# Row power of the last norm: ScalarE's root and a Newton step on VectorE in place of GpSimd's power

## The chip, the cores and the metric

The kernel runs on one core of a Trainium2 chip. A core has five engines with a queue each: TensorE (PE, matmuls; its weight loads are shown apart as PEld), VectorE (DVE), ScalarE (ACT), GpSimd (POOL) and SyncE (SP, which here issues DMAs). The metric is the device time of one execution in microseconds (us), median of several runs.

## The reference

One layer over 256 tokens of width 2048: a gated feed-forward network (hidden width 5632), a mixer (a recurrence and a pooling branch), and a second feed-forward network, each between norms. What matters here is the second network and the norm behind it, which make the output:

```python
def _rmsnorm(x, g):
    xf = x.astype(jnp.float32)
    y = xf * lax.rsqrt(jnp.mean(xf * xf, axis=-1, keepdims=True) + NORM_EPS)
    return (y * g.astype(jnp.float32)).astype(x.dtype)

f = _swiglu(_rmsnorm(h, ln_ffn2_pre[l]), ffn2_gate[l], ffn2_up[l], ffn2_down[l])
h = h + MACARON_WEIGHT * _rmsnorm(f, ln_ffn2_post[l])
```

Each token (a row) needs one number for its last norm: the reciprocal root of the mean square of its 2048 values of `f`. All is float32.

## The kernel before

**Matmuls.** A float32 product is made of three matmuls on split operands: high times high, low times high, high times low (`mm3`, L273 to L275). ScalarE makes the high part by a cast (`wH`, `kH` of weights, `xH` of activations), VectorE the low part by a subtraction (`wL`, `kL`, `xL`). The 256 tokens are two halves of 128 rows (`h` = 0 and 1). Weights stream in by DMAs that SP issues. In most of the blocks some products are joined in the manner of Strassen (`seven`, L458), which takes further sums on VectorE (`t`, `sf`, `u`).

**The order of work.** PE, ACT and DVE instructions stand in an order that the program writes itself: pieces of work are given as jobs with an engine ("A" ScalarE, "V" VectorE, "G" GpSimd, "D" an SP DMA), a planned duration, a due time and what they follow; `play` (L168) runs them against a small model of the engines and emits them in that order. An instruction that an engine reaches early waits for semaphores and holds all behind it on that engine.

**The end of a feed-forward network.** `post` (L996) forms the down projection in blocks of 512 columns and the norm behind it. The evacuation of a block (`ev_of`, L1008) squares and sums its 512 columns on ScalarE (`sumsq`, L845, into `ss[h][:, c]`) and multiplies it by the gain on VectorE (`scale`, L1016, into `fg`). For the first three blocks the sum, times a factor and with epsilon, is made ahead (`some`, L1029 and L1031, `part[h]`, in the profile `rp`). The last block's sums are ordered so that half 0 is done some 11 us before half 1. `last` (L1039) then has, for each half:

- `norm` (VectorE, L1044): `r2 = ss * kf + part`, one number per row; in the profile `rt`
- `power` (GpSimd, L1048): `r = r2 ^ -0.5`; in the profile `rs`
- `out` (VectorE, L1052), four times: `fg * r + residual` for 512 columns each, and behind each one a DMA of 256 KB to the output (SP, L1851)

`post` is called for both feed-forward networks and for the mixer's output, so there are six powers in `post`; two of them (the second network's) stand at the very end. GpSimd's only other work late in the program is DMA issue: the last of these loads the residual (`h<-hsp`, L1830). Behind the last instruction of the program each engine has closing instructions that the compiler adds (a DRAIN, a barrier over all engines); the profile puts them at the line that closes the program, L1895.

**ScalarE's functions.** ScalarE loads a table ahead of some functions (ACT_TABLE_LOAD). Before the change it does so eight times in the program, the last time for the SiLU of the second network (L858, at 1338 us); the kernel has no root on ScalarE.

Of the kernel before, what the change touches and what calls it, by code (L numbers as in the profile page):

```python
# [13 lines left out]
AF = mybir.ActivationFunctionType  # L14
ALU = mybir.AluOpType
# [3 lines left out]
P = 128  # L19
# [4 lines left out]
NKF = DFF // P  # L24
# [27 lines left out]
DOWN = ((0, "fffffffffqffffqfflqlllqllqllqllqlllll", 0),  # L52
        (2, "fffqffqffqffqffqffqflqllqlll", TRAIL))
# [13 lines left out]
class Node:  # L67
    __slots__ = ("n", "eng", "dur", "fn", "due", "lag", "give", "ready", "left", "kids")

    def __init__(s, *a):  # L70
        s.n, s.eng, s.dur, s.fn, s.due, s.lag, s.give = a
        s.ready, s.left, s.kids = 0.0, 0, []
# [8 lines left out]
class Block:  # L81
    def __init__(s, tc, ctx):
        s.tc = tc
        s.nc = nc = tc.nc
        E = ctx.enter_context
        s.n = 0
        s.nxt = None
        s.late, s.after = [], []
        s.clk, s.order, s.asks, s.freed, s.jobs = 0.0, [], {}, {}, []
        s.cp = E(tc.tile_pool(name="cp", bufs=1))  # L90
        s.wp = E(tc.tile_pool(name="wp", bufs=3))
        s.up = E(tc.tile_pool(name="up", bufs=NUNITS))
        s.tp = E(tc.tile_pool(name="tp", bufs=TB))
        s.sp = E(tc.tile_pool(name="sp", bufs=4))
        s.dp = E(tc.tile_pool(name="dp", bufs=1, space=bass.MemoryType.DRAM))
        s.pm = E(tc.tile_pool(name="pm", bufs=4, space=PSUM))
        s.pt = E(tc.tile_pool(name="pt", bufs=4, space=PSUM))
        s.ident = s.const([P, P], "ident")
        make_identity(nc, s.ident)
        s.mhalf = s.const([P, 16], "mhalf")  # L100
        nc.gpsimd.memset(s.mhalf, -0.5)

    def nm(s, p):
        s.n += 1
        return f"{p}_{s.n}"
# [741 lines left out]
    def ffn(s, wg, wu, wd, uT, uj, rs, gpost, resid, emit, reload, xs=None):  # L847
        nc = s.nc
        at = s.T_at(uT)
        nb = NKF // 4  # L850
        hT, hX, hj = [None] * nb, [None] * nb, [None] * nb
        def evs(b, r):
            sig, sj, T1, tj = [None, None], [None, None], [], []

            def silu(h, get, deps, t):
                def f():
                    sig[h] = s.tmp("sg")
                    nc.scalar.activation(out=sig[h], in_=get(), func=AF.Silu, scale=r[h])  # L858
                sj[h] = s.job("A", 0.59, f, t, (*deps, b < 2 and uj[h]))
                return sj[h]  # L860

            def silu_in(h, get, deps, t):
                def f():
                    sig[h] = get()
                    nc.scalar.activation(out=sig[h], in_=sig[h], func=AF.Silu)
                sj[h] = s.job("A", 0.59, f, t, deps)
                return sj[h]

            def turned(h, get, j, t):
                def f():  # L870
                    if not T1:
                        T1.append(s.unit(p="T1"))
                    s.turn(T1[0], h, get())
                tj.append(s.job("V", 0.61, f, t, (j,)))
                if h == 1:
                    hj[b] = s.carry(T1, hT, b, tj, t + 12, None, hX)
                return tj[-1]

            def times(h, get, deps, t):
                def f():  # L880
                    nc.vector.scalar_tensor_tensor(out=sig[h], in0=get(), scalar=r[h],
                                                   in1=sig[h], op0=ALU.mult, op1=ALU.mult)
                j = s.job("V", 0.665, f, t, (*deps, sj[h]))
                turned(h, lambda: sig[h], j, t + 6)
                return j

            def times_in(h, get, deps, t):
                def f():
                    nc.vector.tensor_tensor(out=get(), in0=get(), in1=sig[h], op=ALU.mult)
                j = s.job("V", 0.602, f, t, (*deps, sj[h]))  # L890
                return turned(h, get, j, t + 1)
            return silu, times, silu_in, times_in

        silu, times, _, _ = evs(0, rs)
        if xs:
            pss = s.head(wg, 0, NKD, at, *xs[:2], uT)
            xs[2]()
            for h in range(2):
                s.freed[f"f{h}"] = silu(h, lambda h=h: pss[f"f{h}"], (), 14)
        else:  # L900
            s.lead(wg, 0, at, NKD, silu, lambda k, h: uj[k // 4, h])
        while s.after:
            s.after.pop(0)()
        s.gemm(wu, 0, at, 0, NKD, NKD, times, ("l0", "l1"))
        rb, rj = s.spread(rs, uj)
        nT, nj, nx = s.normed(uT, rb, rj, s.clk + 4, xs and xs[1])
        silu, times, _, _ = evs(1, rs)
        s.gemm(wg, 512, at, 0, NKD, NKD, silu, ("f0", "f1"))
        s.gemm(wu, 512, at, 0, NKD, NKD, times, ("l0", "l1"))
        nq = max(o.count("q") for o in FAST.values())  # L910
        su = Sums(nq)
        t = s.clk + 6
        for q, m in ((0, 2), (2, 1), (3, 1), (4, 1), (5, 1))[:nq - 1]:
            s.sums(nx, su, q, m, t + 4 * q, (nj[q // 2][0],))
        kd = lambda k: (nj[k // 4][1],)
        for b in range(2, nb):
            _, _, silu, times = evs(b, [1.0, 1.0])
            s.seven(wg, b * 512, wu, b * 512, s.T_at(nT), NKD, su, FAST[b], silu, times,
                    kd=kd)
        s.post(wd, s.T_at(hT), NKF, gpost, 0.5, resid, emit, reload, hT, hj, DOWN, hX)  # L920

    def spread_now(s, rs, out):

# [69 lines left out]
            nj.append((b, s.job("V", va(1024), low, t_ + 5, (c,))))  # L993
        return nT, nj, nx

    def post(s, wd, at, KT, gpost, fac, resid, emit, reload, hT, hj, plan, hX=None):  # L996
        nc = s.nc
        gb = [s.unit(p="gb") for _ in range(2)]
        fg = [[s.unit(p="fg") for _ in range(2)] for _ in range(2)]
        ss = [s.small(4, "ss") for _ in range(2)]  # L1000
# [4 lines left out]
        part, sj = [None, None], {}  # L1005
        kf = 1.0 / (D * fac ** 2)

        def ev_of(c):  # L1008
# [30 lines left out]
            def last(h, scale, a, deps, t):  # L1039
                r = s.small(1, "rs", bufs=8)  # L1040
                r2 = s.small(1, "rt2", bufs=2)

                def norm():
                    nc.vector.tensor_scalar(out=r2, in0=ss[h][:, 3:4], scalar1=kf,  # L1044
                                            scalar2=part[h], op0=ALU.mult, op1=ALU.add)

                def power():
                    nc.gpsimd.tensor_tensor(out=r, in0=r2, in1=s.mhalf[:, :1], op=ALU.pow)  # L1048

                def out(q):  # L1050
                    o = cc_(fg[h], q)
                    nc.vector.scalar_tensor_tensor(out=o, in0=o, scalar=r, in1=resid(h, q),  # L1052
                                                   op0=ALU.mult, op1=ALU.add)
                b = s.job("V", 0.13, norm, t, (a, sj[h, "p"]))
                c = s.job("G", 0.55, power, t, (b,), lag=0.35)
                d = s.job("V", 0.602, scale, t + 0.1, deps)
                sj[h, 3] = d
                for q in range(4):
                    o = s.job("V", 0.665, lambda q=q: out(q), t + 0.2 + 0.1 * q, (c, sj[h, q]))
                    emit(h, q, cc_(fg[h], q), o, s.clk + 0.7 + TURNS[h][q])  # L1060
                return s.job("N", 0, None, 0, (a, d))
            return ev
        xj = list(hj)
        if hX is not None:
            c, o, _ = plan[0]
            t, n, first = s.clk, o.count("q"), {}
# [11 lines left out]
        t, q, js = s.clk, 0, []  # L1078
        for c, o, trail in plan:
            n = 0  # L1080
            for ch in o or "p" * (KT // 2) * (1 + (trail > 0)):
# [5 lines left out]
                    n += 1  # L1087
                t += (21 if ch == "q" else 12) * MM
        n1 = None
        for c, o, trail in plan:  # L1090
            if o:
                use = s.seven(wd, c * 512, wd, c * 512 + 512, at, KT, sm, o, ev_of(c),
                              ev_of(c + 1), trail, kd)
                if n1 is None and own is not None:
                    n1 = o.count("q")
                    for q in range(n1, len(sm)):
                        for k in (2 * q, 2 * q + 1):
                            s.link(use[k], js[q // 2])
            elif trail:
                pss = {}  # L1100
                s.gemm(wd, c * 512, at, 0, KT - trail, KT, None, ("l0", "l1"), kd, pss)
                s.halves(wd, c * 512, at, KT - trail, KT, KT, ("l0", "l1"), pss,
                         lambda k, h: kd(k)[0], lambda h, e: ev_of(c)(h, lambda: pss[f"l{h}"],
                                                                   (e,), s.clk))
            else:
                s.gemm(wd, c * 512, at, 0, KT, KT, ev_of(c), ("f0", "f1"), kd)
# [793 lines left out]
```

## Time and profile before

| | |
|---|---|
| time, median of 3 runs | 2015.26 us (2014.19 to 2015.28) |
| profiled execution: its own time | 2014.53 us |
| profiled execution: span, first to last instruction | 2012.8 us |
| time outside the span (2014.53 less 2012.8) | 1.7 us |
| TensorE busy | 1997.0 us (99%) |
| VectorE busy | 1764.8 us (88%) |
| ScalarE busy | 1200.2 us (60%) |
| GpSimd busy | 339.8 us (17%) |

The page of the profile counts matmuls, vector work and the like as busy. Waits, branches, DMA issues and DRAINs are the sequencers' (PEq, ACTq, DVEq, POOLq, SPq) and are not busy time, though they lie within the span. The chain on the page is followed back from the last working instruction, so what stands behind that instruction is in no share of it and has to be looked up by its line, L1895. In a timeline a row has the start and the duration in us; in brackets stands how long the engine had been idle and what released it. In a view by line, three durations are the least, the median and the longest, in ns.

### The profile page before, as it was taken

What the parts mean: (1) busy time and instruction counts of PE and PEld (TensorE: products, weight loads), DVE (VectorE), ACT (ScalarE), POOL (GpSimd) and SP (SyncE); (2) the same over time, 40 slices, a digit from 0 to 9 for tenths busy, and PEclk for the clock granted to TensorE, in tenths of its full rate; (3) what the DMA queues carried; (4) which work ended last, traced back from release to release, by engine and by line L of the source; (5) the groups of instructions that cost most, each with busy time, mean ns of one, the idle gap of its engine ahead of it and who ended that gap; (6) DMA issues with size and microseconds to landing.
All of it is one profiled execution on the core that took longest, in us unless ns stands there. A gap on an engine that the chain in (4) does not pass through costs nothing.

```text
span 2012.8 us, 28601 instructions
## 1 busy us (share of the span) xinstructions
PE 1997.0 (99%) x9936; PEld 1651.9 (82%) x9936; DVE 1764.8 (88%) x2362; ACT 1200.2 (60%) x1599; POOL 339.8 (17%) x689
## 2 busy tenths in 40 slices
PE   9999999999999999999999999999999999999997
PEld 7888888888888888888788788888888888888886
DVE  6999999999998857789689678679999999999885
ACT  7556666566655656775575444565556655756553
POOL 0131112211000113403220120002211131110000
PEclk9999999999999999999999999999999999999999
DMA  9777777766667777757466567766777877666674
GB/s 331 235 217 230 230 242 222 236 185 211 216 205 255 238 203 211 211 176 214 141 182 183 160 218 240 254 219 180 220 228 225 256 218 231 195 215 209 206 258 142
DMA packets 230305, 435.09 MB, mean 216 GB/s; under 512 B 25104, under 2 KB 28688, under 8 KB 230160
## 3 DMA queue, kind: packets, MB, share of 16 engines
q1 hardware_dynamic: 205008, 387.18, 59.9%
q0 software_dynamic: 24864, 45.95, 8.4%
q8 instruction: 78, 1.28, 0.3%
q14 instruction: 67, 0.55, 0.1%
q10 hardware_dynamic: 288, 0.14, 0.0%
HBM read 398.79 MB, written 8.39 MB: 202 GB/s over the span
## 4 chain that ended last, share of the span: by engine, by line
PE 97%; DVE 1%; issue 1%; ACT 1%; DMA 0%; SPq 0%; POOL 0%; DVEq 0%; POOLq 0%; ACTq 0%
PE mm L273 27%; PE mm L275 26%; PE mm L274 26%; PE ms L275 5%; PE ms L274 5%; PE ms L273 5%; PE pA L1596 0%; PE tr L750 0%; DMA w<-in_ffn_gate_dram 0%; PE mc L732 0%; DVE fg L1052 0%; PE pU L1692 0%; DVE wL L298 0%; DVE xL L759 0%; PE pSa L1704 0%
## 5 line engine op out<-in xcount | busy, mean ns | idle before, releaser
L273 PE MATMUL mm<-wH,xH 128*128 128x512 f32 (+1 forms) x1711 | 668.8, 391 | 0.0
L274 PE MATMUL mm<-wL,xH 128*128 128x512 f32 (+1 forms) x1711 | 663.2, 388 | 0.8 <-DVE wL L250 0.8
L275 PE MATMUL mm<-wH,xL 128*128 128x512 f32 (+1 forms) x1711 | 663.4, 388 | 0.3 <-DVE xL L759 0.3
L275 PEld LDWEIGHTS mm<-wH,xL 128*128 128x128 f32 x1711 | 321.2, 188 | 66.8 <-DVE xL L759 0.7
L273 PEld LDWEIGHTS mm<-wH,xH 128*128 128x128 f32 x1711 | 321.3, 188 | 66.3 <-ACT wH L249 0.3
L274 PEld LDWEIGHTS mm<-wL,xH 128*128 128x128 f32 x1711 | 321.5, 188 | 64.6 <-DVE wL L250 1.1
L292 ACT CAST wH<-w 128x1024 fp32r<-128x1024 f32 x251 | 262.6, 1054 | 174.8 <-PE mm L275 122.9
L298 DVE TENSOR_TENSOR wL<-w,wH 128x1024 fp32r<-128x1024 f32 x251 | 301.3, 1218 | 58.3 <-ACT wH L292 56.7
L530 ACT CAST wH<-t 128x1024 fp32r<-128x1024 f32 x163 | 171.8, 1054 | 194.5 <-DVE t L515 69.6
L250 DVE TENSOR_TENSOR wL<-w,wH 128x1024 fp32r<-128x1024 f32 (+2 forms) x159 | 188.2, 1192 | 74.4 <-ACT wH L249 73.0
L781 POOL DMA_DIRECT2D x<-T x352 | 173.3, 511 | 434.4 <-DVE T L768 238.0
L249 ACT CAST wH<-w 128x1024 fp32r<-128x1024 f32 (+2 forms) x159 | 162.7, 1027 | 135.6 <-PE mm L275 113.6
L534 DVE TENSOR_TENSOR wL<-t,wH 128x1024 fp32r<-128x1024 f32 x163 | 196.1, 1216 | 17.3 <-ACT wH L530 17.0
L530 ACT CAST wH<-w 128x1024 fp32r<-128x1024 f32 (+1 forms) x161 | 132.9, 826 | 120.7 <-PE mm L275 68.8
L273 PE MATMUL mm<-kH,xH 128*128 128x512 f32 x449 | 175.5, 391 | 0.0
L275 PE MATMUL mm<-kH,xL 128*128 128x512 f32 x449 | 174.9, 389 | 0.0
L274 PE MATMUL mm<-kL,xH 128*128 128x512 f32 x449 | 174.7, 389 | 0.0
L534 DVE TENSOR_TENSOR wL<-w,wH 128x1024 fp32r<-128x1024 f32 (+1 forms) x161 | 151.1, 938 | 1.1 <-ACT wH L530 1.0
L515 DVE TENSOR_TENSOR t<-w,w 128x1024 f32<-128x1024 f32 x104 | 126.5, 1217 | 6.5 <-DMA w<-in_ffn_down_dram 2.7
L298 DVE TENSOR_TENSOR kL<-w,kH 128x1024 fp32r<-128x1024 f32 x95 | 113.6, 1216 | 6.3 <-ACT kH L292 6.0
L292 ACT CAST kH<-w 128x1024 fp32r<-128x1024 f32 x95 | 98.1, 1048 | 19.5 <-DMA w<-in_ffn_gate_dram 9.3
L275 PEld LDWEIGHTS mm<-kH,xL 128*128 128x128 f32 x449 | 84.3, 188 | 18.0 <-DVE xL L759 0.5
(377 smaller groups left out, 2895.6 us busy)
## 6 DMA issues: line engine op xcount, KB each, us to landing
w<-in_w_in_dram SPq DMA_DIRECT2D x128, 512.0 KB, 4.2
w<-in_ffn_down_dram SPq DMA_DIRECT2D x116, 512.0 KB, 4.7
w<-in_ffn_up_dram SPq DMA_DIRECT2D x104, 512.0 KB, 5.0
w<-in_ffn_gate_dram SPq DMA_DIRECT2D x103, 512.0 KB, 6.1
w<-in_ffn_gate_dram SPq DMA_DIRECT2D x146, 256.0 KB, 4.1
w<-in_ffn_up_dram SPq DMA_DIRECT2D x144, 256.0 KB, 4.1
w<-in_ffn_down_dram SPq DMA_DIRECT2D x120, 256.0 KB, 4.2
w<-in_w_out_dram SPq DMA_DIRECT2D x28, 512.0 KB, 5.9
```

The source lines that it names most:

```text
L249: s.nc.scalar.copy(vH, v)
L250: s.nc.vector.tensor_tensor(out=vL, in0=v, in1=vH.bitcast(F32), op=ALU.subtract)
L273: nc.tensor.matmul(ps, aH, bH, start=start, stop=False)
L274: nc.tensor.matmul(ps, aH, bL, start=False, stop=False)
L275: nc.tensor.matmul(ps, aL, bH, start=False, stop=stop)
L292: s.nc.scalar.copy(b["H"][:, :m], b["t"][:, :m])
L298: s.nc.vector.tensor_tensor(out=b["L"][:, :m], in0=b["t"][:, :m], in1=b["H"][:, :m].bitcast(F32), op=ALU.subtract)
L515: V.tensor_tensor(out=v["t13"], in0=v["a"], in1=v["b0"].to_broadcast([P, 2, 512]), op=ALU.subtract)
L530: nc.scalar.copy(x[n_][0], v[n_])
L534: V.tensor_tensor(out=L, in0=v[n_], in1=H.bitcast(F32), op=ALU.subtract)
L781: nc.gpsimd.dma_start(out=x[0][q * 32:q * 32 + 32, i], in_=src[i * 32:i * 32 + 32, q])
```

## The change

For the last `post` of the program alone (`end` is true where `ffn` is called without the loader of the inputs, which is the second network), `power` is not issued. In its place:

- `root` on ScalarE: the square root of `ss * kf + part`, one number per row, straight from the sum of squares (scale and bias are the instruction's own)
- `better` on VectorE, four instructions on one number per row: the reciprocal `y` of that root, `z = y * y`, `z = z * r2 - 3`, `r = -0.5 * z * y`, which is a Newton step for the reciprocal root
- one root of a constant on ScalarE, some 40 us after the down projection begins in the plan, whose result nothing reads (`sq0`)
- a constant column of 3.0, set by GpSimd at the start

`norm` stays, for the Newton step reads `r2`. Mixer and first network keep GpSimd's power.

```diff
+        s.three = s.const([P, 1], "three")
+        nc.gpsimd.memset(s.three, 3.0)
...
-        s.post(wd, s.T_at(hT), NKF, gpost, 0.5, resid, emit, reload, hT, hj, DOWN, hX)
+        s.post(wd, s.T_at(hT), NKF, gpost, 0.5, resid, emit, reload, hT, hj, DOWN, hX,
+               xs is None)
...
+                def root():
+                    nc.scalar.activation(out=r, in_=ss[h][:, 3:4], func=AF.Sqrt, scale=kf,
+                                         bias=part[h])
+
+                def better():
+                    y, z = [s.small(1, n_, bufs=2) for n_ in ("rt3", "rt4")]
+                    nc.vector.reciprocal(out=y, in_=r)
+                    nc.vector.tensor_tensor(out=z, in0=y, in1=y, op=ALU.mult)
+                    nc.vector.scalar_tensor_tensor(out=z, in0=z, scalar=r2, in1=s.three,
+                                                   op0=ALU.mult, op1=ALU.subtract)
+                    nc.vector.scalar_tensor_tensor(out=r, in0=z, scalar=-0.5, in1=y,
+                                                   op0=ALU.mult, op1=ALU.mult)
                 b = s.job("V", 0.13, norm, t, (a, sj[h, "p"]))
-                c = s.job("G", 0.55, power, t, (b,), lag=0.35)
+                if end:
+                    c = s.job("A", 0.2, root, t, (a, sj[h, "p"]))
+                    c = s.job("V", 0.6, better, t, (b, c))
+                else:
+                    c = s.job("G", 0.55, power, t, (b,), lag=0.35)
...
+        if end:
+            t = s.clk + 40
+            s.job("A", 1.5, lambda: nc.scalar.activation(
+                out=s.small(1, "sq0", bufs=1), in_=s.three, func=AF.Sqrt), t, rel=t - 10)
```

Line numbers shift by up to 24 in the changed program (L1052 becomes L1056, L1895 becomes L1919). The instructions move in three places.

**VectorE, half 1 at the program's end.** `u` is the last block's result, `fg` its product with the gain, `h` the residual. Before:

```order
L573 TENSOR_TENSOR u_18641<-mm_18031,u_18641 128x512 [waits PE_49]
L1016 TENSOR_TENSOR fg_11597<-u_18641,gb_11593 128x512 [waits DVE_49]
L1044 TENSOR_SCALAR rt_7116_11603<-ss_11599,rp_18754 128x1 [waits Activation_49]
L1052 SCALAR_TENSOR_TENSOR fg_11596<-fg_11596,rs_11602,h_2306_432 128x512 [waits DMASW0_49,Pool_49]
L1052 SCALAR_TENSOR_TENSOR fg_11596<-fg_11596,rs_11602,h_2306_432 128x512
```

The same place in the changed program; `rs` comes from ScalarE's root (L1059) and is then overwritten by the Newton step:

```order
L575 TENSOR_TENSOR u_18645<-mm_18035,u_18645 128x512 [waits PE_49]
L1020 TENSOR_TENSOR fg_11599<-u_18645,gb_11595 128x512 [waits DVE_49]
L1048 TENSOR_SCALAR rt_7118_11605<-ss_11601,rp_18758 128x1 [waits Activation_49]
L1064 RECIPROCAL rt_8676_18856<-rs_11604 128x1 [waits Activation_49]
L1065 TENSOR_TENSOR rt_8677_18857<-rt_8676_18856 128x1 [waits DVE_49]
L1066 SCALAR_TENSOR_TENSOR rt_8677_18857<-rt_8677_18857,rt_7118_11605,three 128x1 [waits DVE_49]
L1068 SCALAR_TENSOR_TENSOR rs_11604<-rt_8677_18857,rt_8676_18856 128x1 [waits DVE_49]
L1056 SCALAR_TENSOR_TENSOR fg_11598<-fg_11598,rs_11604,h_2306_434 128x512 [waits DMASW0_49,DVE_49]
L1056 SCALAR_TENSOR_TENSOR fg_11598<-fg_11598,rs_11604,h_2306_434 128x512
```

Four instructions of one column stand between `rt` and the first `fg`, each waiting for the one ahead of it; the wait for Pool is gone. On ScalarE one root stands behind each of the two last `sumsq`.

**GpSimd, its last rows.** Before:

```order
L1011 DMA gb_11593<-in_ln_ffn_post_dram 128x1024 [waits DMASW5_49,DVE_49]
L1830 DMA h_2304_430<-hsp 128x1024 [waits DMAHW0_49,DMASW6_49,DMAHW7_49,DVE_49,Activation_49]
L1830 DMA h_2305_431<-hsp 128x1024 [waits DMASW7_49,DVE_49]
L1830 DMA h_2306_432<-hsp 128x1024 [waits DMASW0_49,DMASW4_49,DVE_49,Activation_49]
L1830 DMA h_2307_433<-hsp 128x1024 [waits DMASW1_49,DVE_49]
L1048 TENSOR_TENSOR rs_11600<-rt_7084_11601,mhalf 128x1 [waits DVE_49]
L1048 TENSOR_TENSOR rs_11602<-rt_7116_11603,mhalf 128x1 [waits DVE_49]
L1895 UNCONDITIONAL_BRANCH
```

And in the changed program:

```order
L1015 DMA gb_11595<-in_ln_ffn_post_dram 128x1024 [waits DMASW5_49,DVE_49]
L1854 DMA h_2304_432<-hsp 128x1024 [waits DMAHW0_49,DMASW6_49,DMAHW7_49,DVE_49,Activation_49]
L1854 DMA h_2305_433<-hsp 128x1024 [waits DMASW7_49,DVE_49]
L1854 DMA h_2306_434<-hsp 128x1024 [waits DMASW0_49,DMASW4_49,DVE_49,Activation_49]
L1854 DMA h_2307_435<-hsp 128x1024 [waits DMASW1_49,DVE_49]
L1919 UNCONDITIONAL_BRANCH
```

Both powers are gone, and GpSimd reaches the program's closing branch, which waits for nothing, behind the last load of the residual.

**ScalarE, early in the down projection.** Casts of weights (`wH`), of the hidden activations (`xH`) and of their sums (`sH`). Before:

```order
L292 CAST wH_17034<-w_8288_16986 128x1024 [waits DVE_49,DMAHW1_49,PE_49,Activation_49]
L530 CAST wH_17051<-w_8289_17005 128x1024 [waits DMAHW2_49,DMAHW3_49,DVE_49,PE_49]
L803 CAST xH_17061<-x_7506_13516 128x4x128 x2
L422 CAST sH_17066<-sf_17054 128x512 [waits DVE_49]
L422 CAST sH_17068<-sf_17054 128x256 [waits DVE_49]
L422 CAST xH_16778<-sf_17054 128x2x128
```

And in the changed program:

```order
L294 CAST wH_17036<-w_8291_16988 128x1024 [waits DVE_49,DMAHW1_49,PE_49,Activation_49]
L1112 ACT_TABLE_LOAD
L1112 ACTIVATE sq_8298_17040<-three 128x1
L532 CAST wH_17062<-w_8292_17007 128x1024 [waits DMAHW2_49,DMAHW3_49,DVE_49,PE_49]
L805 CAST xH_17065<-x_7509_13518 128x4x128
L424 CAST sH_17069<-sf_17055 128x512 [waits DVE_49]
L424 CAST sH_17071<-sf_17055 128x256 [waits DVE_49]
L424 CAST xH_16780<-sf_17055 128x2x128
```

The table load and the unused root come in ahead of a weight cast, and the second of the two `xH` casts goes eight rows down, behind the weight casts of the next group (`wH_17114`). It is the only table load that the change adds: there is none between it and the program's end. The orders of PE and SP are the same, and DVE's is the same but for the end; at the start, on GpSimd, the memset of `three` comes in ahead of the work that makes the identity matrix, and a larger memset goes behind that.

More of the change, by code (lines that the diff above doesn't have):

```diff
@@ L994, in normed, with post @@
         return nT, nj, nx
-    def post(s, wd, at, KT, gpost, fac, resid, emit, reload, hT, hj, plan, hX=None):
+    def post(s, wd, at, KT, gpost, fac, resid, emit, reload, hT, hj, plan, hX=None,
+             end=False):
         nc = s.nc
```

## The prediction

> **What bounds the kernel now.** I read the page first: engines and chain.
>
> ```profile
> PE 1997.0 (99%) x9936; PEld 1651.9 (82%) x9936; DVE 1764.8 (88%) x2362; ACT 1200.2 (60%) x1599; POOL 339.8 (17%) x689
> PE 97%; DVE 1%; issue 1%; ACT 1%; DMA 0%; SPq 0%; POOL 0%; DVEq 0%; POOLq 0%; ACTq 0%
> ```
>
> TensorE sets the time. The change leaves its work alone, so only what lies behind the last matmul can be won: the span of 2012.8 less 2000.55, some 12 us. Next, therefore, the timeline of that end, half 1 of the last norm:
>
> ```profile
> 2000.16 0.39 PE L275 MATMUL mm<-kH,xL 128*128 128x512 f32 x1
> 2000.58 0.69 DVE L573 TENSOR_TENSOR u<-mm,u 128x512 f32<-128x512 f32 x1 [5.76 <-PE mm L275]
> 2001.31 0.69 DVE L1016 TENSOR_TENSOR fg<-u,gb 128x512 f32<-128x512 f32 x1
> 2001.37 0.63 ACT L845 ACTIVATE junk<-u 128x512 bf16<-128x512 f32 x1 [10.21 <-DVE u L573]
> 2001.90 0.19 ACT L845 ACTIVATION_READ_ACCUMULATOR junk<-u 128x1 f32 x1
> 2002.12 0.21 DVE L1044 TENSOR_SCALAR rt<-ss,rp 128x1 f32<-128x1 f32 x1
> 2002.42 0.54 POOL L1048 TENSOR_TENSOR rs<-rt,mhalf 128x1 f32<-128x1 f32 x1 [10.37 <-DVE rt L1044]
> 2003.00 2.74 DVE L1052 SCALAR_TENSOR_TENSOR fg<-fg,rs,h 128x512 f32<-128x512 f32 x4 [0.66 <-POOL rs L1048]
> 2005.77 0.33 SPq L1851 DMA_DIRECT2D out_dram<-fg  x1
> ```
>
> Sum of squares done at 2002.09, power from 2002.42 to 2002.96, outputs from 2003.00, the last DMA issued at 2005.77. It lands 2.6 us later, at 2008.4 (the view of its line). That still leaves 4.4 us to 2012.8, and neither timeline nor chain shows work there. So the view of the closing line, L1895, in two windows: the first four rows are from 2002.3 to 2009, the last from 2012 to 2013. Ahead of them is the landing of the last output's DMA and then of all eight; behind them a piece of the chain with the start of POOL's DRAIN in hundredths, then SP's waits.
>
> ```profile
> DMA to landing us min/median/max: 2.6/2.6/2.6
> DMA to landing us min/median/max: 2.4/2.6/2.7
> ...
> L1895 SPq EVENT_SEMAPHORE  x10: 17/28/28, 2006.1 to 2008.4; - x10
> L1895 SPq DRAIN  x2: 7/7/7, 2008.5 to 2008.6; - x2
> L1895 POOLq DRAIN  x1: 9654/9654/9654, 2002.4 to 2002.4; - x1
> L1895 DVEq DRAIN  x1: 2774/2774/2774, 2003.0 to 2003.0; - x1
> ...
> L1895 POOLq EVENT_SEMAPHORE  x4: 17/17/17, 2012.1 to 2012.7; - x4
> ...
> 2002.38 0.59 POOLq L1895
> ...
> SPq L1895 <- PEq L1895: 4.2, 2, 3.7
> SPq L1895 <- DMA out_dram<-fg: 1.8, 3, 0.9
> ```
>
> SP has seen all landings and has its own DRAIN behind it at 2008.6. DVE's DRAIN ends at 2003.02 + 2.77 = 2005.8. POOL's begins at 2002.38 and takes 9.65 us: to 2012.03, 9.1 us past the end of the power in front of it. At 2012.1 POOL's first barrier semaphore falls, and 0.7 us later the span ends. SP's wait of 3.7 us is put down to PE, which had long been done; what came last is POOL's DRAIN. **The end is bounded by that DRAIN, with SP ready 3.45 us before it** (2012.03 less 2008.58, the middle of what 2008.6 can stand for).
>
> **The change part by part.**
>
> *The DRAIN goes.* Without the two powers POOL's last instruction is the issue of the last residual load:
>
> ```profile
> 1945.44 0.53 POOL L1830 DMA_DIRECT2D h<-hsp  x1 [0.38 <-DVE wL L534]
> L1884 POOLq DRAIN  x1: 179/179/179, 0.4 to 0.4; - x1
> ```
>
> It ends at 1945.97. Behind it the DRAIN may take as little as the 0.18 us of POOL's first DRAIN, which followed memsets, or as much as 9.65: by 1956 it is over, and the matmuls until 2000.5 hide it. Gain at the end: 3.45 us. Late next is SP, whose last output must land; from there to the end the barrier's 0.7 us stay as they are.
>
> *The Trainium skill on the DRAIN.* "Perfetto Trace Analysis", section "Sequencer-only Instruction (DRAIN, etc)", says that the profile counts such an instruction from the point where its semaphores are satisfied, not from the start of its wait. SP's DRAINs of 7 ns, right behind waits for landings, agree. By this rule the 9.65 us are POOL's own doing and no wait for SP, which speaks against the first rival below.
>
> *The new path.* What was 0.91 us from 2002.09 to 2003.00 (norm, power, hand-overs) becomes a root and four column operations in a row. Rows for them, ScalarE's ahead of VectorE's:
>
> ```profile
> L1816 ACT ACTIVATE lc<-mhalf 128x4 f32<-128x4 f32 x1 | 0.2, 205 | 0.0
> L1186 ACT ACTIVATE zt<-R,omu 128x256 f32<-128x256 f32 x1 | 0.5, 497 | 0.0
> L1413 ACT CAST mxT<-pl 128x256 fp32r<-128x256 f32 x8 | 3.2, 403 | 2.5 <-DVE pl L1412 2.4
> L1585 ACT CAST yH<-ident 128x1 fp32r<-128x1 f32 x2 | 0.4, 181 | 0.0
> L754 ACT ACTIVATE xH<-tr,cols 128x128 fp32r<-128x128 f32 x64 | 18.3, 399 | 0.3 <-PE tr L750 0.3
> ...
> L1031 DVE TENSOR_SCALAR rp<-rt 128x1 f32<-128x1 f32 x6 | 0.9, 154 | 0.2
> L1406 DVE TENSOR_TENSOR fx<-pl,rcp 128x1 f32<-128x1 f32 (+3 forms) x8 | 1.3, 160 | 0.0
> L1044 DVE TENSOR_SCALAR rt<-ss,rp 128x1 f32<-128x1 f32 x6 | 1.3, 209 | 0.3
> L406 DVE TENSOR_TENSOR sf<-sf,sx 128x256 f32<-128x256 f32 x1 | 0.4, 424 | 0.0
> ```
>
> The root: 0.205 for a small ScalarE instruction, and for a column as an operand the difference of 497 and 403, 0.09: 0.30. The trace shows no root; its ends are the bare 0.18 of a one-column cast and the 0.40 of 128 elements with a column operand. Reciprocal and square: 0.16 each, by the one-column row they are nearest to. The third reads a column as its scalar, as norm does: 0.21. The fourth has a constant: 0.16. No reciprocal is in the trace; 0.42, a row of 256 elements, is taken as its upper end. Hand-overs are 0.03 to 0.04 (2000.58 + 0.69 to 2001.31; 2001.90 + 0.19 to 2002.12); I take 0.04, and 0.10 as the upper end (2001.27 to 2001.37, VectorE to ScalarE).
>
> Sum: root 2002.12 to 2002.42 (norm, beside it, is done at 2002.33), reciprocal to 2002.62, square to 2002.82, third to 2003.07, fourth to 2003.27, first output at 2003.31. That is **0.31 us later**. Low end: 2002.12 + 0.18 + 4 x (0.03 + 0.15) + 0.03 = 2003.05, 0.05 later. High end: 2002.12 + 0.40 + 0.42 + 0.16 + 2 x 0.21 + 5 x 0.10 = 2004.02, 1.02 later. Outputs, DMA and landing move as one. For half 0 the same 0.31 is hidden: VectorE is idle for 5.76 us ahead of 2000.58.
>
> *The table load and the unused root.* A load is 1.28 us and what follows starts 0.02 behind it. The first two rows are from the program's start; then come ScalarE's timeline and VectorE's where the new pair will stand, and the busy times of PE, PEld, DVE, ACT and POOL from 1780 to 1800, each with its count of instructions:
>
> ```profile
> 1.75 1.28 ACT L1816 ACT_TABLE_LOAD   x1 [1.75 <-PEq L1884]
> 3.05 0.20 ACT L1816 ACTIVATE lc<-mhalf 128x4 f32<-128x4 f32 x1
> ...
> 1784.08 1.05 ACT L292 CAST wH<-w 128x1024 fp32r<-128x1024 f32 x1 [1.07 <-DMA w<-in_ffn_down_dram]
> 1786.14 1.05 ACT L530 CAST wH<-w 128x1024 fp32r<-128x1024 f32 x1 [1.01 <-DMA w<-in_ffn_down_dram]
> 1787.10 1.14 ACT L803 CAST xH<-x 128x512 fp32r<-128x512 f32 x2
> ...
> 1789.13 1.22 DVE L534 TENSOR_TENSOR wL<-w,wH 128x1024 fp32r<-128x1024 f32 x1
> 1792.99 0.69 DVE L534 TENSOR_TENSOR wL<-w,wH 128x512 fp32r<-128x512 f32 x1 [0.16 <-ACT wH L530]
> ...
> 1780.00:1800.00 20.00, 20.00 (x89) 16.55 (x89) 19.81 (x28) 12.74 (x17) 3.98 (x9) 1.00 0.68 216
> ```
>
> By the order the pair stands behind the cast that ends at 1785.13. 1.28 + 0.21 + 0.02 is 1.51 us, of which 1.01 was idle: the next cast starts 0.50 late, at 1786.64, and ends at 1787.69. VectorE takes its low part at 1789.13, so 1.4 us are left. The `xH` cast that goes down takes 0.5 us out of the queue, so what follows is on time again; it comes back near 1793, and ScalarE, busy 12.74 of these 20 us, has room. Cost: 0. If that cover is gone, VectorE (19.81 of 20 busy) and then TensorE (20.00 of 20) are up to 1.5 us late.
>
> "ScalarE: Activation LUTs" of the Trainium skill, section "What ACT_TABLE_LOAD costs", adds a drain of some 1.38 us to each switch, 2.66 in all. By that the cast would be 1.88 late and VectorE's 1.4 us just missed: estimated 0.5 us lost instead of 0; the 0.02 above speaks against it.
>
> *The memset* at the start is an instruction of 0.1 us on POOL ahead of the identity matrix, and a larger one goes behind it; TensorE's warm-up waits for that matrix. I take 0, with 0.1 us to either side.
>
> **The sum.** 3.45 - 0.31 = 3.14 us. The span becomes 2009.7, the profiled execution's own time 2014.53 - 3.14 = 2011.4, and on the median, which is 0.73 above that execution, 2015.26 - 3.14 = 2012.1. That is 0.16%. Faster means by over 0.2% here, 4.03 us, about what a measurement of this kernel can tell from no change. The forecast is therefore **a real gain that counts as the same**. By the bounds (path 0.05 to 1.02, landing 2.4 to 2.7, 0.1 at the start) the gain is 2.3 to 3.6: 2011.7 to 2013.0.
>
> **The rivals.**
>
> *The DRAIN belongs to the end, not to the power.* If POOL's closing waits for something that follows the last landing (2008.4 to 2012.03, 3.7 us), it stays, and the end is later by the 0.31 of the path: 2015.6. For it: it is POOL's only DRAIN after a long program. Against: DVE's, ACT's and SP's ended with their own last work. 5%.
>
> *Slower: the DRAIN costs 9.65 us from when the program closes.* Before, it ran beside outputs and landings. Should it start only when the other engines are through, at 2008.58 + 0.31 = 2008.89, it ends at 2018.54, 6.5 us later than now: 2021.8. It decides as soon as it starts after 2002.38. Against: POOL's branch waits for nothing, and POOL's DRAIN began 0.04 us ahead of its own last instruction, not with the others'. 3%.
>
> *The set is lost again.* Were the table loaded once more ahead of the last root, 1.28 us would lie on the path: gain 1.9, 2013.4. The order has no such load. 3%.
>
> *The table load's cover is gone.* 1.5 us of TensorE: gain 1.6, 2013.6. It decides if a low part that TensorE needs next comes over 1.4 us late. 5%.
>
> *More than the span shows.* If part of the 1.7 us outside the span is POOL's closing too, over 0.9 us more could go: gain over 4.03, below 2011.2. No row speaks for it. 10%.
>
> **How the numbers follow.** Forecast 74%, rivals 5, 3, 3, 5 and 10. The time is that of the forecast, 2012.1. The range runs from 2010.6 (the low bound 2011.7 less 1.1, the spread of the three runs, which takes in half of the last rival) to 2013.7 (lost set and lost cover, 2013.4 and 2013.6); the DRAIN rivals are left out. Faster: the last rival's 10%, and of the forecast's 74% a tenth, where the spread of 1.1 us carries 3.14 over 4.03: 17%. Slower: 3%. Same: 80%.
>
> **What would show it.** Right: POOL's DRAIN starting near 1946 or gone from the end, SP's last DRAIN 0.7 to 0.9 us before the span's end, root near 0.30, column operations 0.16 to 0.21, first output of half 1 some 2.76 us behind the last matmul's end (2000.55 to 2003.31; before 2.45), PE's busy time at 1997. Wrong: a long POOLq DRAIN still last, a table load at the root's line, or new idle time on PE near 1790.

## The result and the profile after

| | before | after |
|---|---|---|
| median of 20 runs each | 2015.03 us (2014.18 to 2016.63) | 2011.57 us (2010.96 to 2013.24) |
| ratio | | 0.9983, 95% interval 0.9976 to 0.9989 |
| profiled execution: own time, span | 2014.53, 2012.8 us | 2012.0, 2010.3 us |
| end of the last matmul to the span's end (from unrounded times) | 12.28 us | 9.05 us |

The time fell by 3.46 us, 0.17%, which is under the 0.2% that the prediction set as the border to "faster", and clear of no change by its interval. The forecast was 3.14 us and 2012.1.

The page first: TensorE's work and the chain's shares are what they were, but for two small terms: "issue" went from 1% to 0%, and POOLq, GpSimd's sequencer, is gone from the chain.

```profile
PE 1997.6 (99%) x9936; PEld 1651.4 (82%) x9936; DVE 1765.9 (88%) x2370; ACT 1201.9 (60%) x1603; POOL 338.6 (17%) x688
PE 97%; DVE 1%; ACT 1%; DMA 0%; issue 0%; SPq 0%; POOL 0%; DVEq 0%; ACTq 0%
```

The timeline of the end, half 1 of the last norm (lines stand up to 24 further down than before):

```profile
2000.86 0.39 PE L277 MATMUL mm<-kH,xL 128*128 128x512 f32 x1
2001.29 0.69 DVE L575 TENSOR_TENSOR u<-mm,u 128x512 f32<-128x512 f32 x1 [5.49 <-PE mm L277]
...
2002.55 0.19 ACT L847 ACTIVATION_READ_ACCUMULATOR junk<-u 128x1 f32 x1
2002.77 0.29 ACT L1059 ACTIVATE rs<-ss,rp 128x1 f32<-128x1 f32 x1
2002.77 0.21 DVE L1048 TENSOR_SCALAR rt<-ss,rp 128x1 f32<-128x1 f32 x1
2003.09 0.16 DVE L1064 RECIPROCAL rt<-rs 128x1 f32<-128x1 f32 x1
2003.29 0.16 DVE L1065 TENSOR_TENSOR rt<-rt 128x1 f32<-128x1 f32 x1
2003.48 0.22 DVE L1066 SCALAR_TENSOR_TENSOR rt<-rt,rt,three 128x1 f32<-128x1 f32 x1
2003.74 0.16 DVE L1068 SCALAR_TENSOR_TENSOR rs<-rt,rt 128x1 f32<-128x1 f32 x1
2003.93 2.74 DVE L1056 SCALAR_TENSOR_TENSOR fg<-fg,rs,h 128x512 f32<-128x512 f32 x4
2004.71 2.32 SPq L1875 DMA_DIRECT2D out_dram<-fg  x4
```

POOL has no row there. From the last matmul's end, 2000.86 + 0.39 = 2001.25, to the first output it is 2.68 us; before it was 2.45 (2000.55 to 2003.00). The new path is 0.23 us longer. What closes the program stands in the view of the closing line, from 1940 to 2009.6:

```profile
L1919 SPq EVENT_SEMAPHORE  x10: 17/28/28, 2007.1 to 2009.4; - x10
L1919 SPq DRAIN  x2: 7/7/7, 2009.5 to 2009.5; - x2
L1919 POOLq DRAIN  x1: 11636/11636/11636, 1946.2 to 1946.2; - x1
...
L1919 POOLq EVENT_SEMAPHORE  x1: 17/17/17, 2009.6 to 2009.6; - x1
```

POOL's DRAIN is not shorter, it is longer: 11.64 us instead of 9.65. But it begins at 1946.2, with the issue of the last load of the residual, and is over at 1957.8, under the matmuls. The last engine ready for the closing barrier is now SP, which has waited for the outputs, at 2009.5. POOL's barrier semaphore falls 0.1 us later, and 0.7 us after that the span ends. SP's waits tell the same: the one of 3.7 us before, put down to PE, is down to 0.5.

```profile
SPq L1919 <- DMA out_dram<-fg: 1.8, 3, 0.9
SPq L1919 <- PEq L1919: 0.7, 2, 0.5
```

Taken by their spans, the two profiled executions differ by 2.5 us, not by 3.2. The rest lies ahead of the end: the last matmul starts at 2000.86 instead of 2000.16. By 12 us TensorE has started 39 matmuls instead of 41, so most of it was lost at the start; another kernel below with the same start (without the early load) has its last matmul end at 2000.51. The start varies that much from one execution to the next, and the ends are compared from the last matmul on.

### The profile page after: what moved, and what is told of

It reads as the page before. It is cut to its first block, busy times and chain, and to the rows that moved or that the text cites. A ratio compares the mean times of both kernels' runs of the same rounds, so it can differ in the third digit from the quotient of the medians.

```text
span 2010.3 us, 28611 instructions
## 1 busy us (share of the span) xinstructions
PE 1997.6 (99%) x9936; PEld 1651.4 (82%) x9936; DVE 1765.9 (88%) x2370; ACT 1201.9 (60%) x1603; POOL 338.6 (17%) x688
## 3 DMA queue, kind: packets, MB, share of 16 engines
q8 instruction: 78, 1.28, 0.3%
## 4 chain that ended last, share of the span: by engine, by line
PE 97%; DVE 1%; ACT 1%; DMA 0%; issue 0%; SPq 0%; POOL 0%; DVEq 0%; ACTq 0%
PE mm L275 27%; PE mm L277 26%; PE mm L276 26%; PE ms L277 5%; PE ms L276 5%; PE ms L275 5%; PE pA L1620 0%; PE tr L752 0%; DMA w<-in_ffn_gate_dram 0%; PE mc L734 0%; DVE fg L1056 0%; PE pU L1716 0%; DVE wL L300 0%; DVE xL L761 0%; PE pSa L1728 0%; PE pY L1751 0%
```

## The experiments

The theory (A): GpSimd's closing DRAIN lasts some 9 to 12 us behind GpSimd's last instruction, whatever that is, and it bounded the end; the change wins because GpSimd's last instruction is now early. The rivals: the time came from the new path or the other order on ScalarE (C); it is the power that leaves a long DRAIN (B); GpSimd's DMAs make it long (D, which the small programs test and which A, as put, leaves open). Times are medians of 11 runs with the ratio to the kernel before on the same chip, where it had 2014.96 us (first four) and 2014.8 (next two).

**The power kept, unused.** In the changed kernel:

```diff
                     c = s.job("V", 0.6, better, t, (b, c))
+                    s.job("G", 0.55, lambda: nc.gpsimd.tensor_tensor(
+                        out=s.small(1, "rt5", bufs=2), in0=r2, in1=s.mhalf[:, :1], op=ALU.pow), t, (b,))
```

> The changed kernel, and GpSimd also takes its power of each half again, into a tile that nothing reads. The output path stays the new one (root, Newton step). Theory A (GpSimd's closing DRAIN lasts some 9 to 12 us behind whatever GpSimd did last, and that bounded the end): the DRAIN starts near its last power again and ends 9 to 10 us behind it, so the span ends some 12.3 us behind the last matmul instead of 9.05, and the time is the one before, 2015.0 (ratio 1.000). Rival C (the time came from the new path or from the other order on ScalarE, not from the DRAIN): the power is off the path, so the time stays at 2011.6 (ratio 0.9983).

2014.74 us, ratio 0.9997 (0.9989 to 1.0006): the gain is gone. The end of its timeline, and then its closing line:

```profile
2000.71 0.39 PE L277 MATMUL mm<-kH,xL 128*128 128x512 f32 x1
...
2002.92 0.54 POOL L1074 TENSOR_TENSOR rt<-rt,mhalf 128x1 f32<-128x1 f32 x1 [10.31 <-DVE rt L1048]
2002.94 0.16 DVE L1064 RECIPROCAL rt<-rs 128x1 f32<-128x1 f32 x1
...
2003.79 2.74 DVE L1056 SCALAR_TENSOR_TENSOR fg<-fg,rs,h 128x512 f32<-128x512 f32 x4
...
L1921 POOLq EVENT_SEMAPHORE  x4: 17/17/17, 2012.6 to 2013.2; - x4
L1921 POOLq DRAIN  x3: 46/98/9656, 2002.9 to 2013.0; - x3
L1921 SPq DRAIN  x3: 7/7/7, 2009.3 to 2012.8; - x3
```

The outputs run as in the changed kernel, 2.69 us behind the last matmul (2001.10), and nobody reads the power. Yet the DRAIN is back at 9.66 us, to 2012.5, and the span ends at 2013.3, 12.2 us behind the last matmul. Rival C is out: as long as the DRAIN stays, the new path and order gain nothing.

**A copy in its place.** The same, with GpSimd copying one column:

```diff
+                    s.job("G", 0.55, lambda: nc.gpsimd.tensor_copy(
+                        out=s.small(1, "rt5", bufs=2), in_=r2), t, (b,))
```

> The same, but in place of the unused power GpSimd copies one column, into a tile that nothing reads, at the same place. Theory A: as with the unused power, a DRAIN of 9 to 12 us at the end, 2015.0 (ratio 1.000). Rival B (it is the power that leaves a long DRAIN behind): the DRAIN is short, under 1 us, the end is 9.05 us behind the last matmul and the time 2011.6 (ratio 0.9983).

2014.57 us, ratio 0.9997 (0.9988 to 1.0006). GpSimd's timeline and the closing line:

```profile
2002.84 0.18 POOL L1074 COPY rt<-rt 128x1 f32<-128x1 f32 x1 [10.69 <-DVE rt L1048]
...
L1921 POOLq DRAIN  x3: 46/98/9274, 2002.8 to 2012.6; - x3
```

The copy is 0.36 us shorter than the power, and the DRAIN is 0.38 shorter, 9.27: 2002.82 + 9.27 is 2012.10 by unrounded times, 9.07 us behind the copy's end. In the kernel before it is 2012.04 less 2002.96, by unrounded times 9.07 as well. So in this kernel the DRAIN ended the same 9.07 us behind a power and behind a copy; rival B is out.

**The table load alone.** The kernel before with the memset, the load and the unused root:

```diff
+        if end:
+            t = s.clk + 40
+            s.job("A", 1.5, lambda: nc.scalar.activation(
+                out=s.small(1, "sq0", bufs=1), in_=s.three, func=AF.Sqrt), t, rel=t - 10)
...
```

> The kernel before, with nothing but the memset, the table load and the unused root of the change. Theory (the cover holds): TensorE has no new idle time near 1786 and the time is the one before, 2015.0, ratio 1.000 within 0.0005. Rival (the 1.5 us of load and root reach TensorE, or the load costs more than its 1.28 us): 2015.5 to 2016.5, ratio 1.0003 to 1.0008, and new idle time of PE near 1790.

2014.63 us, ratio 0.9998 (0.9989 to 1.0007); from the last matmul to the end 12.28 us, as before. ScalarE's timeline, and the busy times from 1780 to 1800 (PE, PEld, DVE, ACT, POOL):

```profile
1784.66 1.06 ACT L294 CAST wH<-w 128x1024 fp32r<-128x1024 f32 x1 [1.35 <-DMA w<-in_ffn_down_dram]
1785.74 1.28 ACT L1096 ACT_TABLE_LOAD   x1
1787.03 0.21 ACT L1096 ACTIVATE sq<-three 128x1 f32<-128x1 f32 x1
1787.14 1.04 ACT L532 CAST wH<-w 128x1024 fp32r<-128x1024 f32 x1
...
1780.00:1800.00 20.00, 20.00 (x90) 16.55 (x89) 19.97 (x28) 13.68 (x19) 4.47 (x10) 1.00 0.70 220
```

TensorE stays at 20.00 of 20. The interval (up to 1.4 us) cannot exclude half a microsecond of loss by time alone. The trace can: from 1330 to 2000 us, which takes in the load, TensorE is busy throughout and does the same 2959 matmuls before and with the load. The kernel before, then the one with the load alone:

```profile
1330.00:2000.00 670.00, 670.00 (x2959) 554.88 (x2958) 620.76 (x726) 391.94 (x455) 98.53 (x192) 1.00 0.68 216
1330.00:2000.00 670.00, 670.00 (x2959) 554.72 (x2958) 621.43 (x726) 394.33 (x457) 98.80 (x192) 1.00 0.68 216
```

**No early load.** The changed kernel without those four lines; the load then stands at half 0's root.

> The changed kernel without the unused root ahead of time; the table load then falls in front of the root of half 0, near 1991.5, where VectorE idles for some 5 us behind half 0's outputs. Theory: half 0's outputs come 1.3 us later, still ahead of half 1, the root of half 1 finds its table; span from the last matmul 9.05 us as in the changed kernel, time 2011.6. Rival (the early load is needed): half 1's path or its DMAs are late by up to 1.3 us, span from the last matmul up to 10.3, time up to 2012.9.

2011.29 us, ratio 0.9983 (0.9974 to 0.9992); 9.04 us from the last matmul to the end. Half 0 in its timeline:

```profile
1991.13 1.28 ACT L1059 ACT_TABLE_LOAD   x1
1992.43 0.29 ACT L1059 ACTIVATE rs<-ss,rp 128x1 f32<-128x1 f32 x1
1992.75 0.16 DVE L1064 RECIPROCAL rt<-rs 128x1 f32<-128x1 f32 x1 [1.39 <-ACT rs L1059]
...
1993.60 2.74 DVE L1056 SCALAR_TENSOR_TENSOR fg<-fg,rs,h 128x512 f32<-128x512 f32 x4
```

VectorE is late by the load's 1.3 us and still through at 1996.3, 4 us ahead of half 1. The early load is of no use here.

**No Newton step.** Root and reciprocal alone:

```diff
                 def better():
+                    nc.vector.reciprocal(out=r, in_=r)
-                    y, z = [s.small(1, n_, bufs=2) for n_ in ("rt3", "rt4")]
...
```

> The changed kernel without the Newton step: root and reciprocal alone (the row factor is then as exact as ScalarE's root). It takes three column operations from the path, by the trace of the changed kernel 0.16 + 0.22 + 0.16 and three hand-overs of 0.035, 0.64 us. Theory (the path and the landing set the end now): the first output of half 1 comes 2.04 us behind the last matmul instead of 2.68, the span ends 8.4 us behind it instead of 9.05, time 2011.0. Rival (something else of the closing ends last, once the DRAIN is gone): the outputs come earlier and the span still ends 9.0 us behind the last matmul, time 2011.6.

2011.09 us, ratio 0.9981 (0.9972 to 0.9990). The last matmul, the first output of half 1 and the closing DRAINs:

```profile
2000.49 0.39 PE L277 MATMUL mm<-kH,xL 128*128 128x512 f32 x1
...
2002.92 2.74 DVE L1056 SCALAR_TENSOR_TENSOR fg<-fg,rs,h 128x512 f32<-128x512 f32 x4
...
L1913 POOLq DRAIN  x3: 46/93/11485, 1945.7 to 2009.0; - x3
L1913 SPq DRAIN  x3: 7/7/7, 2008.5 to 2008.8; - x3
```

The first output is 2.04 us behind the last matmul's end (2000.88) instead of 2.68, the span's end (2009.29) 8.42 behind it instead of 9.05: what is taken from the path comes off the end. With the DRAIN gone, the path sets it.

**The Newton step in two.** The root is taken of four times the mean square, `r2` becomes minus four times it (its parts are made ahead):

```diff
-                    nc.vector.tensor_tensor(out=z, in0=y, in1=y, op=ALU.mult)
-                    nc.vector.scalar_tensor_tensor(out=z, in0=z, scalar=r2, in1=s.three,
-                                                   op0=ALU.mult, op1=ALU.subtract)
-                    nc.vector.scalar_tensor_tensor(out=r, in0=z, scalar=-0.5, in1=y,
-                                                   op0=ALU.mult, op1=ALU.mult)
+                    nc.vector.scalar_tensor_tensor(out=z, in0=y, scalar=r2, in1=y,
+                                                   op0=ALU.mult, op1=ALU.mult)
+                    nc.vector.scalar_tensor_tensor(out=r, in0=z, scalar=3.0, in1=y,
+                                                   op0=ALU.add, op1=ALU.mult)
...
```

> The changed kernel with the Newton step in two instructions behind the reciprocal instead of three (the root is taken of four times the mean square, so that the step's constant goes into one instruction). It takes one column operation and its hand-over from the path, 0.16 + 0.035 = 0.19 us. Theory: first output 2.49 us behind the last matmul instead of 2.68, span 8.86 behind it, time 2011.4. Rival (the merged instruction reads two columns and costs more than what it replaces): 2.68 or more.

The last matmul and the first output of half 1:

```profile
2000.94 0.39 PE L277 MATMUL mm<-kH,xL 128*128 128x512 f32 x1
...
2003.83 2.74 DVE L1066 SCALAR_TENSOR_TENSOR fg<-fg,rs,h 128x512 f32<-128x512 f32 x4
```

By unrounded times the first output is 2.49 us behind the last matmul's end and the span's end 8.87 behind it, as the theory has them (2.49 and 8.86). The time, 2011.75 us and ratio 0.9983 (0.9975 to 0.9992), cannot show 0.2 us. By the trace it is the shorter of the two paths that keep the Newton step.

**What makes the DRAIN long.** Six small programs, run once each, of this pattern, with other counts and sizes of DMAs or, in the first, a power in place of DMAs and copies:

```python
nc.gpsimd.memset(c, -0.5)
...
for k in range(8):
    nc.gpsimd.dma_start(out=w[:, k % 8 * 512:k % 8 * 512 + 512], in_=x[0, :P, k % 4 * 512:k % 4 * 512 + 512])
nc.vector.tensor_copy(d, w)
nc.gpsimd.tensor_copy(out=c, in_=d[:, 4095:])
```

> A small program that leaves the whole computation out and copies x to the output by SP's DMAs; GpSimd does one memset and one power of a column and issues no DMA. Read: the length of GpSimd's closing DRAIN. If the power (theory B) or any last instruction of GpSimd (theory A in its widest form) leaves a long DRAIN: 9 to 12 us. If DMAs that GpSimd issued are what makes it long (theory D): under 0.5 us.

> The same small program, but GpSimd issues eight DMAs, and when they have landed copies one column. Read: the length of its closing DRAIN. Theory D (DMAs that GpSimd issued make it long, whatever comes last): 9 to 12 us. Theory B (the power makes it long): under 0.5 us. Theory A in its widest form: 9 to 12 us.

> The small program with forty DMAs of GpSimd (256 KB each) in place of eight, then the copy of one column. With none the DRAIN ended 0.07 us behind GpSimd's last instruction, with eight 0.74 us. Per-issue theory (0.084 us for each DMA that GpSimd issued): 3.4 us. Fixed-length theory (a step that comes with the first DMAs): 0.7 us.

> The same with 160 DMAs of 256 KB. Per-issue theory: 13.4 us. Capped theory (it grows with the DMAs up to what the large kernel shows): 9.1 us. Fixed-length theory: 0.7 us.

> The same with 160 DMAs of 32 partitions and 32 KB each, the size of most of GpSimd's DMAs in the large kernel. Per-issue theory: as with 160 large ones. Per-packet theory (the DRAIN goes by packets or bytes): a quarter to a half of what 160 large ones take.

> The same with 592 DMAs of 32 KB, about the number that GpSimd issues in the large kernel, where the DRAIN ends 9.07 us behind the last instruction. Capped theory: some 9 us. Per-issue theory without a cap: some 50 us. If it is neither and stays under 2 us, the long DRAIN of the large kernel has a cause that the number of GpSimd's DMAs does not show.

The longest of each row's three durations is the closing DRAIN, in the order of the expectations: none (a power last), 8, 40, 160 large DMAs, 160 small, 592 small.

```profile
L124 POOLq DRAIN  x3: 34/70/652, 6.0 to 13.7; - x3
```
```profile
L127 POOLq DRAIN  x3: 34/95/934, 22.5 to 23.9; - x3
```
```profile
L127 POOLq DRAIN  x3: 34/95/3547, 44.1 to 48.1; - x3
```
```profile
L127 POOLq DRAIN  x3: 40/95/4696, 129.6 to 134.7; - x3
```
```profile
L127 POOLq DRAIN  x3: 40/95/3462, 90.0 to 94.0; - x3
```
```profile
L127 POOLq DRAIN  x3: 40/95/9096, 304.8 to 314.3; - x3
```

Without a DMA of GpSimd's own, the DRAIN behind a power ends with it: 6.03 + 0.65 is 6.68, the power ends at 6.61. With DMAs it ends 0.74, 3.35, 4.50, 3.27 and 8.90 us behind the copy. All of them had landed: the copy reads what VectorE made of their data, and in the program with 592 no packet moves from 302 us to 315, while the DRAIN begins at 304.8 (view of DMA in that window):

```profile
DMA packets 0, 0.00 MB, mean 0 GB/s; under 512 B 0, under 2 KB 0, under 8 KB 0
```

So theory A in its widest form falls: a long DRAIN is no property of any last instruction as such. The rows are as theory D has them: the DRAIN is long where GpSimd has issued DMAs, even when they have landed. The two DRAINs behind the long one, the other two of each row, take 0.03 to 0.10 us, so whatever makes it long is done with once.

Not tested apart from D is what grows along with the DMAs, the length of the program and the number of GpSimd's instructions: no long program was run in which GpSimd works without issuing DMAs. Neither gives the DRAIN's length by itself. The 160 small DMAs are four times as many instructions as the 40 large ones, in a program of 94.2 us instead of 48.4, and the DRAIN is no longer (3.27 and 3.35). The large kernel is over six times as long as the program with 592 (314.6 us), with 9.07 against 8.90.

The law is open. From 8 to 40 DMAs the DRAIN grows by some 0.08 us a DMA, and at 160 it would then be some 13, but is 4.50; small DMAs count for less than large ones at the same number (3.27 against 4.50), yet not a quarter; there is no flat cap below 8.90. The 592 small ones give nearly the large kernel's 9.07, whose 594 (GpSimd's rows in the view of DMA issues, added up) are mostly of that size.

## Why the prediction was right, point by point

- **The DRAIN ends the run.** Right, and tested both ways: with a GpSimd instruction at the end the time is the one before, though the outputs run by the new path. SP was ready 3.47 us ahead of the DRAIN's end (2008.57 and 2012.04); the forecast took 3.45. Its 2008.58 is not the middle of what 2008.6 can stand for, which is 2008.60, but the trace has 2008.57.
- **Behind the last DMA issue the DRAIN takes 0.18 to 9.65 us.** Too low by its upper end: 11.64. It cost nothing, since the matmuls go on for 43 us behind its end.
- **The new path, 0.31 us longer.** 0.23. The root took 0.294 us for 0.30, the column operations 0.16, 0.16, 0.22 and 0.16 as taken; the hand-overs were 0.03 to 0.04 instead of 0.04. The reciprocal, for which no row stood, cost 0.16 like the others.
- **The table load costs nothing.** Right. In the changed kernel the cast behind it starts 2.48 us after the cast ahead of it (1785.12 and 1787.60), before 2.06: 0.42 late, where 0.50 was taken. TensorE's busy time from 1780 to 1800 stayed at 20.00, and its matmuls from 1330 to 2000 are 2959 as before. The drain of 1.38 us that the Trainium skill ("ScalarE: Activation LUTs", "What ACT_TABLE_LOAD costs") adds to a switch shows in no row: the root starts 0.01 us behind the load (1785.74 + 1.28 and 1787.03 in the kernel with the load alone). The measurement decides.
- **A DRAIN that belongs to the end** and **one that starts when the program closes**: both out, since it starts at 1946.2, with POOL's last instruction, and is over 52 us ahead of the end. The Trainium skill's rule on the start of such a row ("Perfetto Trace Analysis", "Sequencer-only Instruction (DRAIN, etc)") pointed that way, and the trace agrees.
- **The set lost again**: no load stands at the last root. **More than the span shows**: the time outside the span is 1.7 us as before (2012.0 less 2010.3).
- **The memset, 0.1 us to either side.** TensorE's first matmul starts at 1.61 us instead of 1.72, and by 12 us the profiled execution has lost that again; in the time it does not show.
- **The size.** From the last matmul to the end 12.28 became 9.05, 3.23 against 3.14, and the two terms account for it: 3.47 less 0.23. No error was cancelled by another; both terms came out somewhat better than taken. That the medians differ by 3.46 adds nothing to this, since their interval (2.2 to 4.8 us) takes in 3.23. The gain's bounds of 2.3 to 3.6 leave out the 0.1 at the start that stands beside them; with it they are 2.2 to 3.7.

## What to carry to other kernels

When the chain on a page ends some microseconds ahead of the span, look up the closing line. GpSimd's DRAIN counted here from GpSimd's last instruction, so one tiny operation late on an engine with a long DRAIN can move the end: a copy of 0.18 us cost the 3 us that the change wins. Where GpSimd has issued many DMAs, as in this kernel, let it do its last work early; what is needed late is better done, even if it takes more instructions, on an engine whose DRAIN ends with its work, here ScalarE and VectorE (0.04 and 0.05 us behind it in the changed kernel). What a table load costs is to be sought in the idle time next to it, and tested alone.

## What the runs showed of the hardware

GpSimd's closing DRAIN was longer in programs in which GpSimd had issued more DMAs, all of them landed: it ended 0.07 us behind GpSimd's last instruction with none, 0.74 with 8 of 256 KB, 3.35 with 40 and 4.50 with 160 of these, 3.27 with 160 of 32 KB, 8.90 with 592 of these. It was 9.07 in four programs of the large kernel (before, power kept, copy kept, load alone), where the last DMA had been issued 57 us earlier, so that waiting had not worn it off. Behind a DMA issue as the last instruction it was longer, 11.64 us from the DRAIN's start in the changed kernel. The law behind these lengths is open. A root of one column with a column as bias took ScalarE 0.294 us and a reciprocal of one column VectorE 0.164.
